# Moving the conditioning of layer B's gate from quarter 2 into quarter 1's output stage, in a two-layer fp32 decoder trunk

## The chip, the cores and the metric

The kernel runs on one core of one Trainium2 chip. The metric is the device time of one execution in microseconds (us), the median over several runs. The engines are named as the profile names them: PE is TensorE's matmul, PEld its weight load, DVE is VectorE, ACT is ScalarE, POOL is GpSimd, and SP is SyncE, whose queue issues every DMA of this kernel. TensorE's granted clock was 0.999 of full speed over the profiled execution, which is the 2.4 GHz level.

## The reference, cut to what matters

Layer A is a gated MLP with spatial mixing inside chunks of 128 tokens, layer B is dilated attention over a shared K/V. Both are conditioned by one vector `c`: a shift, a scale and a gate come from `silu(c) @ ada_w + ada_b`. This case is about layer B's gate, the last third of that product.

```
D_MODEL, SEQ, BATCH = 1024, 2048, 1

def ada_mod(c, w, b, n):
    h = jax.nn.silu(c) @ w + b
    return jnp.split(h[:, None, :], n, axis=-1)

def dilated_layer(x, c, kv_groups, ada_w, ada_b, norm_g, w_in, q_norm_g, w_out):
    shift, scale, gate = ada_mod(c, ada_w, ada_b, 3)
    h = rms_norm(x, norm_g) * (1 + scale) + shift
    ...
    y = o.reshape(bsz, s, B_WIDTH) * jax.nn.silu(z)
    return x + gate * (y @ w_out)
```

The gate of layer B is a row of 1024 numbers: a product of a vector of 1024 with a 1024 x 1024 block of `b_ada_w` (4.19 MB in fp32), plus a bias.

## The kernel before

The 2048 tokens are worked through in four quarters of 512 (`Q` = 0 to 3 in the code; "quarter 1" is `Q` = 0). Each quarter runs layer A and then the projections of layer B:

- the v blocks, with a gelu, then a spatial mix;
- the u and the z blocks (`dense_f`, 256 columns at a time);
- the output stage: `dense` over `a_w_out` in quarter 1, where each of two column halves `n` is made in two passes of 8 weight tiles (`kh`), so four passes in all. In later quarters it is a Strassen-like product, `dense_s`. Its result is gated, added to x, normalised and transposed;
- `proj_B`: the products for k and v (`kv_block` 2, 1, 0) and for q and z.

Dense work is in fp32r: each weight tile is loaded raw (`raw_o` and its like, 256 KB), ACT copies its high part into `w_o`, DVE subtracts that from the raw tile to get the low part (line 262), and PE runs three matmuls of 128x512 for each pair of tiles. There are 8 such split tiles (pool `wp`) and 6 raw ones (pool `rp`).

Beside the dense work run *fillers*: Python generators that emit side work in slices, in turn. `tick(part)` stands after each weight tile and adds `rate[0] * part` slices to a counter; `fill` pops the first generator of a list, advances it by one `yield` and puts it at the end. So the rate and the number of fillers set how fast each one is emitted. What is emitted is then ordered on each engine by a list scheduler at compile time: instructions keep a priority by the order in which they were emitted, a tile waits for a free buffer of its tag, and each engine, and SP's DMA queue, then runs its list strictly in order.

The fillers that matter here:

- `side_work` (quarter 1): layer A's gate, the shifts and scales, and `combine_weights` for layer B's input weights. It ends about where the output stage of quarter 1 begins.
- `combine_v` (quarter 1, from the output stage on): for 8 values of `k` it loads four 256 KB tiles of v's weights (line 378), combines them with four DVE subtractions (lines 382 to 385) and stores them to `wv` (line 256). Its tiles lie in the attention's buffers (`pr`, `pT`, `qt`, `qT`), which are idle until quarter 2. It takes 36 slices. `wv` is first read in quarter 2's v blocks.
- `attend_local` (from quarter 2 on): attention of groups 1 and 0 for the quarter before, and `combine_weights((4, 5), True)` for the output weights.
- `ada_gate(..., 1, "gb")`: layer B's gate. For each of two column halves `h`, `ada_acc` loads four tiles of 512 KB of `b_ada_w` (line 175) and accumulates eight 128x512 products on DVE (lines 177 and 179) into a tile of tag `ev` (pool `ep`, 6 buffers); six idle slices later PE sums over partitions (line 232, a 128x512 fp32 matmul with one stationary column), DVE adds the bias row (line 233) and SP stores the row to `gd`. One half is 10 slices, so the whole is 20. `gate_out`, in quarter 3, is the first to read it.

In quarter 2 the gate is woven into `attend_local`: `weave(main, side)` advances `side` once with each slice of `main`, and it has no slices of its own as long as `main` lasts. Its weight tiles take turns with the attention's `kv` tiles in pool `xp` (tag `xin`, 4 buffers).

Of the kernel before, what the change touches and what calls it, by code (L numbers as in the profile page):

```python
# [12 lines left out]
F32 = mybir.dt.float32  # L13
F32R = mybir.dt.float32r
AF = mybir.ActivationFunctionType
ALU = mybir.AluOpType
AX = mybir.AxisListType

P = 128
D = 1024  # L20
# [14 lines left out]
def trunk(ctx, tc, out, x, c, a_ada_w, a_ada_b, a_norm_g, a_w_in, a_sgu_g, a_w_spatial,  # L35
          a_b_spatial, a_w_out, kv_ada_w, kv_ada_b, kv_norm_g, w_kv, k_norm_g, b_ada_w,
          b_ada_b, b_norm_g, b_w_in, b_q_norm_g, b_w_out, dbg=None):
    nc = tc.nc
# [11 lines left out]
    xp = ctx.enter_context(tc.tile_pool(name="xp", bufs=4))  # L50
# [4 lines left out]
    ap_ = ctx.enter_context(tc.tile_pool(name="ap", bufs=2))  # L55
# [10 lines left out]
    wt = [[dp.tile([512, 512], F32, name=f"wt{b}_{i}") for i in range(4)] for b in range(4)]  # L66
# [8 lines left out]
    fillers = []  # L75
# [13 lines left out]
    rate = [0, 0]  # L89
# [7 lines left out]
    def drain():  # L97
        while fillers:
            fill(1)

    def evt(name, dt=F32):
        return ep.tile([P, 512], dt, tag="ev", name=name)

    def pst(name, tag="a"):
        return ps.tile([P, 512], F32, tag=tag, name=name)
# [26 lines left out]
    sc = cp.tile([P, KT], F32, name="sc")  # L132
# [33 lines left out]
                            channel_multiplier=-1)  # L166


    def ada_acc(res, w, c0, nm):

        acc = evt(f"acc_{nm}")
        for k in range(KT):
            if k % 2 == 0:
                wt = xp.tile([P, 2, 512], F32, tag="xin", name=f"aw_{nm}{k}")
                nc.sync.dma_start(wt, w[k * P:(k + 2) * P, c0:c0 + 512].rearrange("(k p) n -> p k n", p=P))
            if k == 0:
                nc.vector.tensor_scalar(acc, wt[:, 0, :], sc[:, 0:1], None, ALU.mult)
            else:
                nc.vector.scalar_tensor_tensor(acc, wt[:, k % 2, :], sc[:, k:k + 1], acc, ALU.mult, ALU.add)
            if k % 2:  # L180
                yield
        res.append(acc)
# [39 lines left out]
    def ada_gate(w, b, i, nm):  # L222
        for h in range(2):
            res = []
            cs = slice(h * 512, (h + 1) * 512)
            yield from ada_acc(res, w, 2 * D + h * 512, f"{nm}{h}")
            yield from [None] * (3 if i else 1)
            row = evt(f"gr_{nm}{h}")[0:1, :]
            nc.sync.dma_start(row, b[:, 2 * D + h * 512:2 * D + (h + 1) * 512])
            yield from [None] * 3  # L230
            pg = pst(f"pg_{nm}{h}")
            nc.tensor.matmul(pg[0:1, :], ones, res[0], start=True, stop=True)
            nc.vector.tensor_tensor(row, pg[0:1, :], row, ALU.add)
            nc.sync.dma_start(gd[i:i + 1, cs], row)
# [170 lines left out]
    def idle(n, gen):  # L405

        for _ in range(n):
            yield
        yield from gen

    def weave(main, side):

        for _ in main:
            next(side, None)
            yield
        for _ in side:
            yield
# [91 lines left out]
    def sum_tile(nm):  # L509
        return tp.tile([P, 516], F32, tag="st", name=f"st_{nm}")  # L510
# [492 lines left out]
    def layer_A(Q, hA, m, sqv, us=None, sums=None):  # L1003
# [69 lines left out]

        if Q == 0:
            fillers.append(combine_v())
            rate[0] = 1.6
        xts = []
        for t in range(TPQ):
            xt = xp.tile([P, D], F32, tag="xin", name=f"xr{Q}_{t}")
# [413 lines left out]
    def attend_local(Q, wrap=False):  # L1493

        bs = range(4 * Q, 4 * Q + 4)
        yield from attend([(1, b) for b in bs], wrap)
        v = stat[1][:, 4 * Q:4 * Q + 4, :]
        nc.sync.dma_start(std[1].rearrange("(n i r) c -> i n r c", n=4, r=4)[:, Q], v)
        yield
        nc.sync.dma_start(v, std[1].rearrange("(b i) c -> i b c", i=P)[:, 4 * Q:4 * Q + 4])  # L1500
        yield from attend([(0, b) for b in bs], wrap, 3)
# [205 lines left out]
    for Q in range(NQ):  # L1707
        if Q > 0:
            main = attend_local(Q - 1, True)
            if Q == 1:  # L1710
                fillers.append(weave(main, idle(12, ada_gate(b_ada_w[0], b_ada_b, 1, "gb"))))
                fillers.append(idle(8, combine_weights((4, 5), True)))
            else:
                fillers.append(weave(main, idle(16, gate_out())) if Q == 2 else main)
            rate[0] = 1.8 if Q == 1 else 0.6
        if Q == 0:
            with in_order(behind=True):
                hk, hb, keep, tail = layer_A(Q, hA, m, sqv, first)
        else:
            hk, hb, keep, tail = layer_A(Q, hA, m, sqv, sums=sums)  # L1720
        if Q > 0:
            drain()
        nxt = {}

        def ahead(Q=Q):
            if Q + 1 < NQ:
                fillers.append(make_hA(nxt, Q + 1, affa))
                rate[0] = 1.1
            else:
                nxt["fin"] = finish()  # L1730
            return nxt.get("fin")
        proj_B(Q, hk, hb, keep, tail, ahead)
        if Q + 1 < NQ:
            drain()
            hA, sums = nxt["hA"], nxt.get("ops")
            m, sqv = v_tiles(Q + 1)
# [23 lines left out]
```

## Time and profile before

| what | value |
|---|---|
| median of 3 runs | 2903.24 us (2902.45 to 2907.31) |
| the profiled execution | 2904.99 us |
| its span, first to last instruction | 2903.3 us |
| PE busy | 2875.6 us (99%) |
| PEld busy | 2419.2 us (83%) |
| DVE busy | 2219.1 us (76%) |
| ACT busy | 1667.6 us (57%) |
| DMA traffic | 693.82 MB, 239 GB/s over the span |

The profiled execution's own time is its span and 1.7 us around it. A busy PE need not be PE at its peak, since the ends of matmuls are modelled; so the count of matmuls in a stretch is read beside its busy time.

### The profile page before, as it was taken

Reading aid. Unit: us, or ns where it says so; the run is one execution under the profiler, and the core shown is the slowest. Engines: PE = TensorE matmul, PEld = TensorE weight load, DVE = VectorE, ACT = ScalarE, POOL = GpSimd, SP = SyncE. Lnnn points to the kernel's source line nnn. Section 1 sums busy time; section 2 is a strip of 40 time slices with the busy share of each in tenths; the row PEclk is TensorE's granted clock in tenths of the full one; section 3 lists DMA queues with packets and bytes.
Section 4 is the critical chain, followed back from the end, with each engine's and each line's share of the span. In section 5 each row is a group of like instructions: output and inputs, shape, how many; then the busy total and the mean of one; then the engine's idle time right before and its main releaser. Section 6 shows DMA issues by size and latency. Waiting matters only on the chain. (4 is left out here: it accounts for less than half of the span.)

```text
span 2903.3 us, 44921 instructions
## 1 busy us (share of the span) xinstructions
PE 2875.6 (99%) x14610; PEld 2419.2 (83%) x14610; DVE 2219.1 (76%) x4246; ACT 1667.6 (57%) x3400; POOL 258.2 (9%) x549
## 2 busy tenths in 40 slices
PE   8999999999999999999999999999999999999999
PEld 5888888888888888888888888888888888988887
DVE  6786677787758986887878876987678876888972
ACT  4423345668456765676555665676355667876540
POOL 1000001101011000000010000000010003311100
PEclk9999999999999999999999999999999999999999
DMA  7899788777998577776676676766554667889842
GB/s 258 298 311 297 265 287 292 241 250 249 311 334 284 171 259 225 239 247 201 212 262 198 192 253 212 243 225 197 172 174 155 223 219 238 269 265 340 260 144 87
DMA packets 390783, 693.82 MB, mean 239 GB/s; under 512 B 42027, under 2 KB 119821, under 8 KB 390549
## 3 DMA queue, kind: packets, MB, share of 16 engines
q1 hardware_dynamic: 390548, 690.97, 72.3%
q8 instruction: 115, 1.88, 0.3%
q14 instruction: 120, 0.98, 0.1%
HBM read 530.97 MB, written 159.85 MB: 238 GB/s over the span
## 5 line engine op out<-in xcount | busy, mean ns | idle before, releaser
L306 PE MATMUL pd_kv<-w_kv,hkh 128*128 128x512 f32 x768 | 238.5, 391 | 0.3 <-DMA w_kv<-wk 0.2
L355 PE MATMUL pd_u<-hAh,w_u 128*128 128x512 f32 x512 | 207.8, 406 | 0.0
L355 PE MATMUL pd_z<-hAh,w_z 128*128 128x512 f32 x512 | 205.8, 402 | 0.0
L1423 ACT ACTIVATE pr<-pr,stat,rt 128x256 f32<-128x256 f32 (+1 forms) x320 | 177.4, 556 | 45.3 <-DVE stat L1420 30.0
L357 PE MATMUL pd_u<-hAh,w_u 128*128 128x512 f32 x512 | 200.6, 392 | 1.7 <-DVE w_u L262 1.7
L357 PE MATMUL pd_z<-hAh,w_z 128*128 128x512 f32 x512 | 200.4, 392 | 0.0
L356 PE MATMUL pd_u<-hAl,w_u 128*128 128x512 f32 x512 | 200.0, 391 | 0.0
L356 PE MATMUL pd_z<-hAl,w_z 128*128 128x512 f32 x512 | 199.8, 390 | 0.0
L306 PEld LDWEIGHTS pd_kv<-w_kv,hkh 128*128 128x128 f32 x768 | 143.3, 188 | 30.1 <-ACT w_kv L260 0.6
L1484 PEld LDWEIGHTS po<-kv,pT 128*128 128x128 f32 x1200 | 147.6, 191 | 7.4 <-ACT pT L1321 1.2
L1484 PE MATMUL po<-kv,pT 128*128 128x128 f32 x1200 | 149.8, 275 | 1.0 <-ACT pT L1321 1.0
L306 PE MATMUL pd_kv<-w_kv,hkl 128*128 128x512 f32 x384 | 149.8, 390 | 0.0
L1351 POOL TENSOR_SCALAR rt<-qt 128x4 f32<-128x4 f32 x96 | 26.8, 279 | 1311.9 <-DMA qt<-qd 724.7
L1413 DVE SCALAR_TENSOR_TENSOR pr<-dist,rt,ps 128x256 f32<-128x256 f32 (+1 forms) x320 | 124.7, 431 | 22.4 <-PE ps L1409 10.4
L260 ACT ACTIVATE w_u<-raw_u 128x512 fp32r<-128x512 f32 x96 | 59.5, 628 | 142.4 <-PE pd_u L357 95.2
L260 ACT ACTIVATE w_o<-raw_o 128x512 fp32r<-128x512 f32 x104 | 64.2, 628 | 96.4 <-PE pd_o L306 37.8
L260 ACT ACTIVATE w_q<-raw_q 128x512 fp32r<-128x512 f32 x144 | 88.6, 628 | 49.9 <-PE pd_kv L306 9.9
L357 PEld LDWEIGHTS pd_u<-hAh,w_u 128*128 128x128 f32 x512 | 96.1, 188 | 23.9 <-DVE w_u L262 2.9
L357 PEld LDWEIGHTS pd_z<-hAh,w_z 128*128 128x128 f32 x512 | 96.1, 188 | 21.0
L355 PEld LDWEIGHTS pd_u<-hAh,w_u 128*128 128x128 f32 x512 | 96.5, 188 | 18.4 <-issue 1.7
L356 PEld LDWEIGHTS pd_z<-hAl,w_z 128*128 128x128 f32 x512 | 96.5, 188 | 17.6
L355 PEld LDWEIGHTS pd_z<-hAh,w_z 128*128 128x128 f32 x512 | 96.4, 188 | 17.4
(866 smaller groups left out, 7944.8 us busy)
## 6 DMA issues: line engine op xcount, KB each, us to landing
raw_q<-in_b_w_in_dram SPq DMA_DIRECT2D x144, 256.0 KB, 3.8
w_z<-wuz SPq DMA_DIRECT2D x64, 512.0 KB, 4.3
raw_o<-in_a_w_out_dram SPq DMA_DIRECT2D x104, 256.0 KB, 3.5
qt<-qd SPq DMA_DIRECT2D x96, 258.0 KB, 3.6
raw_v<-in_a_w_in_dram SPq DMA_DIRECT2D x96, 256.0 KB, 4.0
raw_u<-in_a_w_in_dram SPq DMA_DIRECT2D x96, 256.0 KB, 5.3
od<-ot SPq DMA_DIRECT2D x96, 256.0 KB, 2.5
raw_kv<-in_w_kv_dram SPq DMA_DIRECT2D x76, 256.0 KB, 4.7
```

Source lines behind the costliest of these rows:

```text
L260: nc.scalar.activation(hi, src, AF.Copy)
L306: last_mm[0] = nc.tensor.matmul(pt, a, u[:, w, :], start=f, stop=e, skip_group_check=more)
L355: nc.tensor.matmul(pts[i], wh, hh[:, k, :], start=k == 0, stop=False)
L356: nc.tensor.matmul(pts[i], wh, hl[:, k, :], start=False, stop=False)
L357: nc.tensor.matmul(pts[i], wl, hh[:, k, :], start=False, stop=k == KT - 1)
L1351: nc.gpsimd.tensor_scalar(rt[:, 12:16], u["qt"][:, 512:516], 1.0 / P, EPS, ALU.mult, ALU.add)
L1413: nc.vector.scalar_tensor_tensor(pr[:, i, :], dist3[:, d0:d0 + w], u["rt"][:, h:h + 1], psc[:, i, :], ALU.mult, ALU.add)
L1423: nc.scalar.activation(pr[:, i, :], pr[:, i, :], AF.Exp, bias=mneg[:, i:i + 1], scale=u["rt"][:, h:h + 1], accum_out=lsum[:, i:i + 1])
L1484: nc.tensor.matmul(po[:, h * P:(h + 1) * P], u["pT"][h // hp][:, h % hp, j, :], u["kv"][:, j, kh, 1, :], start=j == 0, stop=j == nk - 1)
```

## The change

Layer B's gate is no longer woven into quarter 2's attention. It becomes a filler of its own in quarter 1's output stage, behind four idle slices, beside `combine_v`, and the rate there rises from 1.6 to 3.8. Its weight tiles no longer come from `xin`: those of `k` = 0 and 4 go into the attention's `kT` tile (one buffer, 128x2x512, unused until quarter 2), those of `k` = 2 and 6 into two `st` tiles each (pool `tp`, 8 buffers), loaded by two DMAs of 256 KB in place of one of 512 KB.

```
-    def ada_acc(res, w, c0, nm):
+    def ada_acc(res, w, c0, nm, late_tile=False):
 
         acc = evt(f"acc_{nm}")
         for k in range(KT):
             if k % 2 == 0:
-                wt = xp.tile([P, 2, 512], F32, tag="xin", name=f"aw_{nm}{k}")
-                nc.sync.dma_start(wt, w[k * P:(k + 2) * P, c0:c0 + 512].rearrange("(k p) n -> p k n", p=P))
+                src = w[k * P:(k + 2) * P, c0:c0 + 512].rearrange("(k p) n -> p k n", p=P)
+                if late_tile and k % 4:
+                    ws = [sum_tile(f"aw_{nm}{k}{i}")[:, 0:512] for i in range(2)]
+                    for i in range(2):
+                        nc.sync.dma_start(ws[i], src[:, i, :])
+                else:
+                    wt = ap_.tile([P, 2, 512], F32, tag="kT", bufs=1, name=f"aw_{nm}{k}") if late_tile else \
+                        xp.tile([P, 2, 512], F32, tag="xin", name=f"aw_{nm}{k}")
+                    nc.sync.dma_start(wt, src)
+                    ws = [wt[:, i, :] for i in range(2)]
             if k == 0:
-                nc.vector.tensor_scalar(acc, wt[:, 0, :], sc[:, 0:1], None, ALU.mult)
+                nc.vector.tensor_scalar(acc, ws[0], sc[:, 0:1], None, ALU.mult)
             else:
-                nc.vector.scalar_tensor_tensor(acc, wt[:, k % 2, :], sc[:, k:k + 1], acc, ALU.mult, ALU.add)
+                nc.vector.scalar_tensor_tensor(acc, ws[k % 2], sc[:, k:k + 1], acc, ALU.mult, ALU.add)
             if k % 2:
                 yield
         res.append(acc)
@@ ada_gate
-            yield from ada_acc(res, w, 2 * D + h * 512, f"{nm}{h}")
+            yield from ada_acc(res, w, 2 * D + h * 512, f"{nm}{h}", i > 0)
@@ layer_A
         if Q == 0:
             fillers.append(combine_v())
-            rate[0] = 1.6
+            fillers.append(idle(4, ada_gate(b_ada_w[0], b_ada_b, 1, "gb")))
+            rate[0] = 3.8
@@ the loop over quarters
             if Q == 1:
-                fillers.append(weave(main, idle(12, ada_gate(b_ada_w[0], b_ada_b, 1, "gb"))))
+                fillers.append(main)
                 fillers.append(idle(8, combine_weights((4, 5), True)))
```

## Rows read from the trace of the kernel before

**Rows 1.** The page: busy time of each engine, and GB/s in 40 equal slices.
```profile
span 2903.3 us, 44921 instructions
PE 2875.6 (99%) x14610; PEld 2419.2 (83%) x14610; DVE 2219.1 (76%) x4246; ACT 1667.6 (57%) x3400; POOL 258.2 (9%) x549
...
GB/s 258 298 311 297 265 287 292 241 250 249 311 334 284 171 259 225 239 247 201 212 262 198 192 253 212 243 225 197 172 174 155 223 219 238 269 265 340 260 144 87
```

**Rows 2.** Busy time by stretch: two passes, output stage, kv_block 2, quarters 2 and 4.
```profile
core 0: us, PE busy (x) PEld busy (x) DVE busy (x) ACT busy (x) POOL busy (x), PEclk, DMA share, GB/s
320.20:342.00 21.80, 21.80 (x98) 18.06 (x97) 16.75 (x27) 7.84 (x14) 0.00 (x0) 1.00 0.93 303
342.00:363.80 21.80, 21.80 (x98) 18.06 (x97) 8.15 (x13) 6.17 (x12) 0.00 (x0) 1.00 0.37 119
320.20:407.20 87.00, 87.00 (x393) 72.04 (x392) 50.84 (x82) 26.36 (x51) 2.40 (x4) 1.00 0.72 244
407.20:440.00 32.80, 32.25 (x150) 26.26 (x149) 31.81 (x57) 25.07 (x52) 2.94 (x4) 1.00 0.92 311
620.00:820.00 200.00, 197.30 (x1004) 163.82 (x1003) 151.35 (x271) 131.12 (x266) 14.84 (x26) 1.00 0.85 288
1860.00:2060.00 200.00, 200.00 (x1041) 170.21 (x1040) 160.41 (x309) 135.66 (x261) 17.03 (x34) 1.00 0.63 205
```

**Rows 3.** Waits of PE, 300 to 620 us and 620 to 820 us: total, times, longest.
```profile
PE pt_b L656 <- DVE xr L1106: 0.5, 1, 0.5
...
PE pd_u L357 <- DVE w_u L262: 1.7, 2, 1.0
PE pd_v10a L306 <- DVE w_v L262: 1.0, 2, 0.8
```

**Rows 4.** Instructions of lines 175, 177, 179, 232: ns min/median/max, first and last start.
```profile
L175 SPq DMA_DIRECT2D aw_gb<-in_b_ada_w_dram x8: 379/404/462, 647.3 to 774.1; - x8
DMA to landing us min/median/max: 3.8/5.6/9.9
L177 DVE TENSOR_SCALAR acc_gb<-aw_gb,sc x2: 478/478/478, 699.1 to 766.6; 128x512 f32<-128x512 f32 x2
L179 DVE SCALAR_TENSOR_TENSOR acc_gb<-aw_gb,sc,acc_gb x14: 731/740/752, 702.1 to 781.4; 128x512 f32<-128x512 f32 x14
L232 PE MATMUL pg_gb<-acc_gb,ones x4: 590/591/592, 764.1 to 810.6; 128*1 128x512 f32 x4
```

**Rows 5.** Timeline of quarter 2, 715 to 727 us: start, duration, idle before and releaser.
```profile
721.21 0.75 DVE L179 SCALAR_TENSOR_TENSOR acc_gb<-aw_gb,sc,acc_gb 128x512 f32<-128x512 f32 x1 [3.63 <-DMA aw_gb<-in_b_ada_w_dram]
...
725.67 0.69 DVE L262 TENSOR_TENSOR w_u<-raw_u,w_u 128x512 fp32r<-128x512 f32 x1
...
726.42 0.50 PE L357 MATMUL pd_u<-hAh,w_u 128*128 128x512 f32 x1 [1.00 <-DVE w_u L262]
```

**Rows 6.** Timeline of quarter 1's output stage, PE and DVE: start, duration, idle before.
```profile
320.19 0.61 PE L306 MATMUL pd_o<-w_o,yh 128*128 128x512 f32 x2
...
341.95 0.61 PE L306 MATMUL pd_o<-w_o,yh 128*128 128x512 f32 x2
342.81 0.69 DVE L262 TENSOR_TENSOR w_o<-raw_o,w_o 128x512 fp32r<-128x512 f32 x1 [0.62 <-ACT w_o L260]
...
366.27 0.68 DVE L262 TENSOR_TENSOR w_o<-raw_o,w_o 128x512 fp32r<-128x512 f32 x1
...
377.80 0.69 DVE L382 TENSOR_TENSOR co<-co,co 128x512 f32<-128x512 f32 x1 [7.56 <-DMA co<-in_a_w_in_dram]
378.41 0.68 DVE L262 TENSOR_TENSOR w_o<-raw_o,w_o 128x512 fp32r<-128x512 f32 x1
```

**Rows 7.** Waits of SP's DMA queue, 300 to 500 us, the first.
```profile
SPq L267 <- DVE w_o L262: 32.3, 18, 11.8
```

**Rows 8.** Instructions on combine_v's tiles of odd k: ns min/median/max, first and last start.
```profile
L378 SPq DMA_DIRECT2D co<-in_a_w_in_dram x16: 327/565/1212, 322.9 to 462.4; - x16
L382 DVE TENSOR_TENSOR co<-co,co x4: 681/688/692, 331.0 to 466.7; 128x512 f32<-128x512 f32 x4
```

## The prediction, made before the change was run

> **What bounds the kernel now.** I read the page first: PE is busy for 2875.6 of 2903.3 us, DVE for 2219.1 [rows 1]. A busy PE may still be a slow one, so I went to the busy times by stretch. The reader should see there that PE's pace does not depend on the side work: the first pass of quarter 1's output stage holds 98 matmul records in 21.8 us while DVE is busy for 16.75 us and the DMA engines for 0.93 of the time, and the second holds the same 98, with the same 18.06 us of weight loads, while DVE is busy for 8.15 us and DMA for 0.37 [rows 2]. The clock is 1.00 throughout, the 2.4 GHz level. So PE is the bound, and a change beside it can give back only what PE loses to waits, or add to it.
>
> Hence the list of PE's waits, for the stretch that gains work and the one that loses it. From 300 to 620 us it names one, of 0.5 us; in the output stage itself, 320.2 to 407.2 us, PE is busy for all 87.00 us [rows 2, 3]. From 620 to 820 us, where the gate lies now, it names 2.7 us in four waits, all on DVE's low parts of weights (line 262), and PE is idle there for 200 - 197.30 = 2.7 us too [rows 2, 3]. That is the whole prize in quarter 2. The bound I use for a change that can be measured here is 0.2%, 5.8 us.
>
> **What is removed.** The gate's work in quarter 2 is 8 loads of 512 KB (0.40 us of SP's queue each, landing after 5.6 us, 9.9 at most), 2 x 0.48 + 14 x 0.74 = 11.3 us of DVE, and two PE products, each of two records of 0.59 us [rows 4]. DVE is busy for 151.35 of 200 us there [rows 2], so its time lies in gaps; what can reach PE is a wait. The timeline shows one: DVE stood 3.63 us for a gate tile until 721.21 us, the split behind it came at 725.67, and PE waited for a split from 725.4 to 726.42 us, 1.00 us [rows 5]. The other 1.7 us have no such stop in front of them in these rows: 1.0 is in v's blocks, 0.7 is the second wait of u's [rows 3]. So I take -1.0 us, with 0 and -2.7 as ends: 0 if another late tile takes the gate's place in front of the split, -2.7 if a lighter queue cures all four. That `kv` tiles find `xin` free sooner I cost at nothing: no wait of PE there names the attention. Its slices of emission stay as they are, since `weave` gave the gate none of its own.
>
> **What is added in quarter 1.** The two PE products move with the rest and cost the same: 0. The loads become 4 of 512 KB and 8 of 256 KB, so four more issues at about 0.4 us of SP's queue, 1.6 us; the bias rows and their stores move unchanged. DVE gets the gate's 11.3 us. The slices: the stage has 64 ticks of 0.25, so 64 x 0.25 x 3.8 = 60.8 in place of 25.6. The gate needs 4 + 20 and one to end, and `side_work` has some 5 left: a third each of the first 15 slices, then half each, so the gate ends after 15 + 40 = 55 slices, inside the stage. `combine_v` gets 5 + 20 + 5, about 30, in place of 25.6 - 5, about 20: 10 more, or 2.5 values of `k`: 2.5 x 4 x 0.69 = 6.9 us of DVE [rows 8] and 2.5 x 2.1 = 5.2 MB, drawn forward out of the projections.
>
> DVE in the stage: 50.84 + 11.3 + 6.9 = 69 of 87 us [rows 2]. It fits. DMA: 87 us at 244 GB/s is 21.2 MB; with 4.2 and 5.2 it is 30.6 MB, or 352 GB/s, above the fastest fortieth of the span, 340 [rows 1, 2]. So the stage fills the DMA engines, and some 1 MB spills past its end, 3 us. What hides this is the lead of the weights. The passes begin at 320.19 and 341.95 us, 21.76 apart, and each works through its 8 tiles in the first 10.9 us, 1.36 us a tile. The last split of the second pass's tiles is ready at 343.5 us and wanted at 341.95 + 7 x 1.36 = 351.5: a lead of 8.0 us. The third pass begins at 363.7, its last split is ready at 366.95 and wanted at 373.2: 6.3 us [rows 6]. And a wait of the new kind has been there without harm: DVE stood 7.56 us for a tile of `combine_v`, the split behind it came at 378.41, was ready at 379.1, and was wanted at 385.5 [rows 6]. I take 0 for the stage, between 0 (all waits stay inside the lead, as that one did) and +9.8 us (worked out under the second rival).
>
> Behind the stage, in `kv_block` 2, DVE is busy for 31.81 of 32.8 us and PE idle for 0.55 [rows 2]. `combine_v` leaves it in part, so I take -0.5 us; the ends are -0.55 and, if half of the gate (5.7 us of DVE) were late enough to land there instead, 5.7 - 0.99 = +4.7 us.
>
> **The sum.** -1.0 + 0 + 0 - 0.5 = -1.5 us on the profiled execution's 2904.99, so 2903.5. The median of the runs is 1.75 us under that execution; as a median I predict 2903.24 - 1.5 = 2901.7 us.
>
> **Rivals.** *The first: Quarter 2 gains more than its named waits.* The share of weight loads is 163.82 of 200 us there and 170.21 in quarter 4's same blocks [rows 2]. If all of the difference were lost pace, 6.4 us at 0.851 per us is 7.5 us, and the median 2903.24 - 7.5 - 0.5 = 2895.2. Against it: quarter 4 has a different attention, so another mix of matmuls, and the two passes above kept their 18.06 us at very different loads. The Trainium skill ("Trainium Kernel Development and Optimization", Performance Expectations) says that matmul busy time misleads and that the busy share of weight loads is the measure; by that rule the 83% would leave room, and the time would be this rival's. The equal counts of the two passes speak against reading it so here.
>
> *The second, and the other side: a late gate tile holds the splits.* The place is DVE's list in the output stage. SP's queue stands up to 11.8 us at a time until a raw buffer is free, 32.3 us in 18 waits [rows 7]. A gate load queued behind such a wait, and landing after 9.9 in place of 5.6 us [rows 4], comes 11.8 + 4.3 = 16.1 us late; DVE stands for it, the splits stand behind it, and PE loses what is beyond the lead: 16.1 - 6.3 = 9.8 us. It decides from a wait of 6.3 us on. The single `kT` buffer makes it likelier: `k` = 4 can't be loaded until `k` = 1 has been used, and SP stands for that with the raw loads behind it. The median would be 2901.7 + 9.8 = 2911.5. For it: the 7.56 us wait, already over the smallest lead; in quarter 2 the same tiles made a stop of 3.63 us. Against it: that wait cost nothing, and the second pass has 13.65 us of free DVE. The Trainium skill ("TensorE: Matmul & The Clock Gate", the section on the 16 sub-arrays) gives VectorE a strictly ordered queue of 8. The split that came 0.6 us after the held subtraction agrees; by that rule the change moves a stop, it doesn't dissolve it.
>
> *The third: the move is less than it says.* The list scheduler may place the gate's second half in `kv_block` 2, where DVE has 0.99 us free: -1.0 + 4.7 = +3.7, so 2906.9. It is inside 0.2%. Any new order of the lists elsewhere (PE's whole idle time is 2903.3 - 2875.6 = 27.7 us over the span [rows 1]) I count into the spread.
>
> **How the numbers follow.** Forecast 0.72; larger gain 0.08; late tile 0.12; half move 0.08. The range: the forecast's own ends are -2.7 - 0.55, so 2900.0, and with the 0.8 us between the two lower runs 2899.2; above, 2906.9 is the third rival. For the cases beyond I open it to 2898 and 2909, which takes in a small version of each. Faster by over 0.2% is the first rival, 0.08; slower is the second, 0.12; the forecast and the third rival are within, 0.80.
>
> **What would show it.** Right: no `acc_gb` after some 405 us, PE's 1.00 us wait at 726 us gone, PE busy for all of the output stage with 393 records in 87 us, DVE near 69 us there, DMA share over 0.9. Wrong: waits of PE on `w_o` in the output stage, behind a stop of DVE over 6.3 us on an `aw_gb` tile; or `acc_gb` beside `kv_block` 2 and PE waiting for `hkl` or `w_kv`; or quarter 2's weight loads rising toward 170 us in 200.

## The result, and the profile after

The change made the kernel slower: a median of 2924.66 us (2921.49 to 2929.91, 6 runs) against 2906.72 us for the kernel before in the same comparison (2902.45 to 2907.31, 6 runs, the three of the table of before among them). The ratio is 1.0068, with a 95% interval of 1.0055 to 1.0081. The prediction was 2901.7 us, with a range from 2898 to 2909. In the new file the lines up to 1073 stand 8 lower and the later ones 9 lower: the low part of a weight is line 270, the matmul of `dense` is line 314, `combine_v`'s four subtractions are lines 390 to 393.

The head of the page answers to [rows 1]:

```profile
span 2921.6 us, 44949 instructions
PE 2883.1 (99%) x14610; PEld 2422.2 (83%) x14610; DVE 2221.7 (76%) x4246; ACT 1670.4 (57%) x3400; POOL 263.2 (9%) x549
```

The span grew by 18.3 us. PE's idle time went from 27.7 to 2921.6 - 2883.1 = 38.5 us, so 10.8 of them are waits. The other 7.5 us are PE being busy for longer over the same 14610 instructions. The busy times by stretch say where (columns as in [rows 2]):

```profile
320.00:340.00 20.00, 14.90 (x57) 11.80 (x57) 15.20 (x26) 4.67 (x9) 0.00 (x0) 0.86 0.95 316
340.00:360.00 20.00, 20.00 (x87) 16.47 (x86) 9.59 (x15) 5.06 (x8) 0.00 (x0) 0.97 0.84 272
...
400.00:420.00 20.00, 16.45 (x72) 13.41 (x71) 10.96 (x19) 4.27 (x9) 2.56 (x4) 0.91 0.93 342
620.00:820.00 200.00, 200.00 (x1018) 169.14 (x1017) 151.37 (x268) 139.60 (x278) 13.91 (x26) 1.00 0.86 287
```

Two things are new in quarter 1's output stage: PE is idle, and the granted clock is below 1.00. Over 20 us that is a mean; in two shorter stretches the granted clock was 0.50, the level of 1.2 GHz:

```profile
334.50:341.30 6.80, 5.80 (x14) 4.55 (x15) 5.92 (x10) 1.63 (x3) 0.00 (x0) 0.50 0.85 260
416.50:419.90 3.40, 3.40 (x13) 2.81 (x12) 1.70 (x3) 0.63 (x1) 0.00 (x0) 0.50 0.61 211
```

At 1.00 the stage's rate is 90 records in 20 us (98 in 21.8 us, [rows 2]). The first two rows hold 57 + 87 = 144 in place of 180, which is 36 x 0.222 = 8.0 us. PE's waits from 300 to 470 us answer to the one of 0.5 us in [rows 3]:

```profile
PE pd_o L314 <- DVE w_o L270: 5.1, 1, 5.1
PE pt_b L664 <- DVE xr L1115: 3.5, 1, 3.5
```

So of the 8.0 us 5.1 are the wait and 2.9 the slower clock, which is half of the 5.80 busy us at 0.50. The second wait is 3.5 us, and half of 3.40 busy us at 0.50 is 1.7 us more. Quarter 2, in the last row of the stretches, has lost its idle time: 200.00 us busy in place of 197.30.

What stood ahead of the first wait is in the timeline of DVE, with PE's matmul that ended it:

```profile
324.04 0.69 DVE L390 TENSOR_TENSOR co<-co,co 128x512 f32<-128x512 f32 x1 [1.06 <-DMA co<-in_a_w_in_dram]
324.64 1.28 DVE L270 TENSOR_TENSOR w_o<-raw_o,w_o 128x512 fp32r<-128x512 f32 x2
329.33 0.69 DVE L391 TENSOR_TENSOR co<-co,co 128x512 f32<-128x512 f32 x1 [3.40 <-DMA co<-in_a_w_in_dram]
329.94 3.70 DVE L1078 TENSOR_TENSOR yl<-mt,yh 128x512 fp32r<-128x512 f32 x6
333.55 1.28 DVE L1071 TENSOR_TENSOR mt<-mt,z 128x512 f32<-128x512 f32 x2
334.76 0.68 DVE L270 TENSOR_TENSOR w_o<-raw_o,w_o 128x512 fp32r<-128x512 f32 x1
...
335.50 0.79 PE L314 MATMUL pd_o<-w_o,yh 128*128 128x512 f32 x1 [5.10 <-DVE w_o L270]
```

The reader is to see which tile DVE stood for: `co`, a tile of `combine_v`, and not one of the gate's. Behind it stood 5 us of other work (lines 1078 and 1071), which stands ahead of that split in the kernel before too, and behind that the last split of the first pass. The second wait has the same kind of cause; these are DVE's rows ahead of the scaled rows `xr` that PE transposes:

```profile
403.64 0.69 DVE L390 TENSOR_TENSOR co6pr<-co6pr,co6pr 128x512 f32<-128x512 f32 x1 [4.59 <-DMA co6pr<-in_a_w_in_dram]
...
413.18 0.69 DVE L390 TENSOR_TENSOR co<-co,co 128x512 f32<-128x512 f32 x1 [3.06 <-DMA co<-in_a_w_in_dram]
...
415.14 0.75 DVE L1115 TENSOR_SCALAR xr<-xr,r_b 128x1024 f32<-128x1024 f32 x1
```

The gate itself ran as predicted. Its instructions by line answer to [rows 4], and its last product on DVE begins at 389.2 us, before the forecast's 405:

```profile
L187 DVE SCALAR_TENSOR_TENSOR acc_gb<-st_aw_gb,sc,acc_gb x8: 744/750/752, 339.1 to 389.2; 128x512 f32<-128x512 f32 x8
L187 DVE SCALAR_TENSOR_TENSOR acc_gb<-aw_gb,sc,acc_gb x6: 744/750/754, 337.6 to 387.6; 128x512 f32<-128x512 f32 x6
L240 PE MATMUL pg_gb<-acc_gb,ones x4: 590/590/591, 384.5 to 423.2; 128*1 128x512 f32 x4
```

**Four stretches, all kernels.** One profiled execution varies, so the table splits each by the first matmul of a tile: "stage" from the first of `pd_o` to the first of `pd_kv`, "behind" from there to the first of `pd_q00a`, "quarter 2" from `pd_v10a` to `pd_o1a`, "later" from `pd_o1a` to `pf`, in us. The ratio is that of the timed runs, against runs of the kernel before in the same comparison. Names are those of the experiments below.

| kernel | stage | behind | quarter 2 | later | ratio (95%) |
|---|---|---|---|---|---|
| before | 88.9 | 144.3 | 318.7 | 1674.1 | |
| after | 104.7 | 143.5 | 312.2 | 1682.3 | 1.0068 (1.0055 to 1.0081) |
| gate alone, rate 1.6 | 92.5 | 147.6 | 312.1 | 1672.8 | 1.0002 (0.9991 to 1.0013) |
| rate 3.8 alone | 99.2 | 144.2 | 316.7 | 1681.7 | 1.0060 (1.0042 to 1.0078) |
| no gate | 90.8 | 144.4 | 312.1 | 1672.8 | 0.9981 (0.9972 to 0.9990) |
| combine_v 6 slices later | 94.3 | 145.4 | 313.0 | 1679.5 | 1.0028 (1.0018 to 1.0038) |
| remainder alone | 89.3 | 145.5 | 315.8 | 1677.5 | 1.0042 (1.0025 to 1.0058) |
| remainder set back | 106.3 | 143.4 | 313.1 | 1672.2 | 1.0046 (1.0029 to 1.0063) |
| first pass at 1.6 | 101.1 | 144.8 | 312.4 | 1673.8 | 1.0041 (1.0026 to 1.0056) |
| late combine_v and gate | 94.0 | 144.8 | 312.1 | 1670.5 | 1.0007 (0.9998 to 1.0017) |
| after, combine_v on POOL | 100.6 | 143.6 | 312.2 | 1678.0 | 1.0050 (1.0035 to 1.0066) |
| the same, remainder set back | 101.1 | 145.4 | 312.1 | 1673.3 | 1.0032 (1.0020 to 1.0043) |
| before, combine_v on POOL | 89.0 | 147.6 | 315.8 | 1673.7 | 1.0019 (1.0009 to 1.0029) |
| gate alone, combine_v on POOL | 90.6 | 152.3 | 312.1 | 1671.4 | 1.0009 (0.9999 to 1.0018) |
| no k = 1 subtractions | 104.8 | 143.5 | 312.2 | 1681.3 | 1.0071 (1.0056 to 1.0086) |
| gate twice per slice | 91.4 | 143.4 | 314.0 | 1675.3 | 1.0000 (0.9991 to 1.0010) |
| old pace of combine_v | 97.0 | 144.7 | 311.9 | 1670.6 | 1.0021 (1.0011 to 1.0030) |

The stage has the same order of instructions on DVE and SP in "before", "no gate" and "remainder alone": 88.9, 90.8 and 89.3 us, so it is read to about 2 us. Nor is the profiled run always near the median of its kernel: with the remainder alone it took 2911.10 us (median 2918.38), with the old pace of `combine_v` 2903.39 (2908.74), with the gate twice per slice 2907.81 (2903.65). After against before: +15.8 in the stage, -0.8 behind it, -6.5 in quarter 2, +8.2 later. With what lies between, it makes the 18.3 us of the span.

### The profile page after: what moved, and what is told of

The parts are those of the page before. It is cut to its first block, busy times and chain, and to the rows that moved or that the text cites. A ratio compares the mean times of both kernels' runs of the same rounds, so it can differ in the third digit from the quotient of the medians.

```text
span 2921.6 us, 44949 instructions
## 1 busy us (share of the span) xinstructions
PE 2883.1 (99%) x14610; PEld 2422.2 (83%) x14610; DVE 2221.7 (76%) x4246; ACT 1670.4 (57%) x3400; POOL 263.2 (9%) x549
## 4 chain that ended last, share of the span: by engine, by line
PE 78%; DMA 9%; DVE 6%; ACT 3%; issue 2%; SPq 1%; POOL 0%; DVEq 0%; ACTq 0%; POOLq 0%
PE pd_kv L314 9%; PE po L1493 4%; PE pd_u L363 4%; PE pd_u L365 4%; PE pd_u L364 4%; PE pd_z L363 3%; PE pd_z L365 3%; PE pd_z L364 3%; PE pd_v L314 2%; PE pm L1038 2%; PE pf L1689 2%; PE pf L1688 2%; PE pf L1687 2%; PE pd_o3a L314 1%; PE pd_o2b L314 1%
## 5 line engine op out<-in xcount | busy, mean ns | idle before, releaser
L365 PEld LDWEIGHTS pd_u<-hAh,w_u 128*128 128x128 f32 x512 | 96.1, 188 | 20.8
L364 PEld LDWEIGHTS pd_u<-hAl,w_u 128*128 128x128 f32 x512 | 96.5, 189 | 17.1
```

The lines of the kernel that those rows point to most:

```text
L364: nc.tensor.matmul(pts[i], wh, hl[:, k, :], start=False, stop=False)
L365: nc.tensor.matmul(pts[i], wl, hh[:, k, :], start=False, stop=k == KT - 1)
```

## The experiments

**1. The two halves of the change by themselves.** The first kernel has the gate in the new place at the old rate, the second the new rate with the gate left in quarter 2.

```
+            fillers.append(weave(combine_v(), idle(4, ada_gate(b_ada_w[0], b_ada_b, 1, "gb"))))
             rate[0] = 1.6
```
```
             fillers.append(combine_v())
-            rate[0] = 1.6
+            fillers.append(idle(24, iter(())))
+            rate[0] = 3.8
```

> The gate moves into the output stage and the attention's buffers as in the change, but the rate stays at 1.6 and the gate is woven into the combining of v's weights, so that this keeps the slices it had before. Theory A (the higher rate pulls the combining's subtractions ahead of weight splits; the gate itself is harmless): no wait of PE on a weight split near 330 us and none on the normalised rows near 415, quarter 1 ends within 2 us of before, quarter 2 gains some 5 us, and the time is between 2898 and 2906, ratio 0.997 to 1.001. Theory B (the gate's own tiles and traffic hold the splits): waits of PE of 3 us or more in the output stage with gate instructions in front of the split, and 8 us or more over before.

> The gate stays in quarter 2 as before; in the output stage the rate is 3.8 and an empty filler of 24 slices takes the turns that the gate would have had, so that the combining of v's weights runs at the changed kernel's pace without the gate. Theory A: the same wait of some 5 us near 330 us behind a subtraction that waits for its load, quarter 1 some 8 to 15 us longer than before, and since quarter 2's gain is missing, 10 to 20 us over before (ratio 1.003 to 1.007). Theory B: quarter 1 within 2 us of before, the time within 0.2% of before.

Measured: 2906.21 us (ratio 1.0002) for the gate, 2923.99 us (1.0060) for the rate. The rate alone is about as slow as the changed kernel, without a gate in the stage. Its DVE and its PE show the same kind of stop:

```profile
333.58 0.69 DVE L383 TENSOR_TENSOR co<-co,co 128x512 f32<-128x512 f32 x1 [4.70 <-DMA co<-in_a_w_in_dram]
...
339.00 0.68 DVE L262 TENSOR_TENSOR w_o<-raw_o,w_o 128x512 fp32r<-128x512 f32 x1
...
339.74 0.80 PE L306 MATMUL pd_o<-w_o,yh 128*128 128x512 f32 x1 [6.73 <-DVE w_o L262]
```

In the stage the rate costs 99.2 - 88.9 = 10.3 us and the gate 92.5 - 88.9 = 3.6; both together cost 15.8, which is 1.9 us more and within the 2 us to which the stage is read. With the gate alone quarter 2 is 6.6 us shorter too; the kernel comes out level because its stage is 3.6 us longer and the stretch behind it 3.3 (147.6 in place of 144.3). The reason for the rate's cost is in the order in which the compiled program lists DVE's work; the trace of each kernel has DVE's instructions in that order. These are the kernel before (first) and after (second), from the fifth split of the first pass to its last; the numbers are places in the list:

```
358 L262 TENSOR_TENSOR w_o_0_4_2850<-raw_o_0_4_2851,w_o_0_4_2850 128x512
359 L262 TENSOR_TENSOR w_o_0_5_2855<-raw_o_0_5_2856,w_o_0_5_2855 128x512
360 L262 TENSOR_TENSOR w_o_0_6_2860<-raw_o_0_6_2861,w_o_0_6_2860 128x512
361 L1070 TENSOR_TENSOR yl_2418<-mt_1_1121,yh_2417 128x512 x6
362 L1063 TENSOR_TENSOR mt_1_1121<-mt_1_1121,z_14_2805 128x512
363 L1063 TENSOR_TENSOR mt_1_1121<-mt_1_1121,z_15_2810 128x512
364 L262 TENSOR_TENSOR w_o_0_7_2865<-raw_o_0_7_2866,w_o_0_7_2865 128x512
```
```
358 L270 TENSOR_TENSOR w_o_0_4_2850<-raw_o_0_4_2851,w_o_0_4_2850 128x512
359 L390 TENSOR_TENSOR co_2990<-co_2991,co_2990 128x512
360 L270 TENSOR_TENSOR w_o_0_5_2855<-raw_o_0_5_2856,w_o_0_5_2855 128x512
361 L270 TENSOR_TENSOR w_o_0_6_2860<-raw_o_0_6_2861,w_o_0_6_2860 128x512
362 L391 TENSOR_TENSOR co_2991<-co_2992,co_2991 128x512
363 L1078 TENSOR_TENSOR yl_2418<-mt_1_1121,yh_2417 128x512 x6
364 L1071 TENSOR_TENSOR mt_1_1121<-mt_1_1121,z_14_2805 128x512
365 L1071 TENSOR_TENSOR mt_1_1121<-mt_1_1121,z_15_2810 128x512
366 L270 TENSOR_TENSOR w_o_0_7_2865<-raw_o_0_7_2866,w_o_0_7_2865 128x512
```

The higher rate emits `combine_v`'s `k` = 1 earlier, and two of its subtractions come to stand ahead of `w_o_0_7`. Before, all four stood behind it.

**2. No gate at all, and combine_v held back.** The first kernel shows what is to be had at most; it leaves the gate of layer B out. The second is the changed kernel with six idle slices ahead of `combine_v`.

```
-            fillers.append(idle(4, ada_gate(b_ada_w[0], b_ada_b, 1, "gb")))
-            rate[0] = 3.8
+            rate[0] = 1.6
```
```
-            fillers.append(combine_v())
+            fillers.append(idle(6, combine_v()))
```

> Layer B's gate is not computed at all (the gated output weights take layer A's gate row in its place); everything else, rate included, is as before. This prices what leaving quarter 2 can give at most, under both theories: between -7 and 0 us against before, with PE's losses between 620 and 820 us down from some 5 us to 1. If it is slower than before, or if later quarters lose several us, then the order of later instruction lists moves the time by itself, whatever is taken out.

> The change with one addition: the combining of v's weights starts six slices later, so that none of its subtractions stands ahead of the first pass's last weight split. Theory A: the wait of 5.1 us near 330 us is gone and the clock stays at 1.00 there, 8 us less than the changed kernel in that pass; the second stop, near 412 us, may stay, since the combining still runs at the high rate. So 2908 to 2918. Theory B: the gate's own instructions stand where they stood, so both stops stay, 2920 or more.

Measured: 2900.25 us (0.9981) without a gate, and 2913.53 us (1.0028) with `combine_v` later. So all of the gate's work is worth 0.19%, some 5.5 us, and that is the most that any place for it could give. The gate's products take 2.4 us of PE in any place, so if PE stays the bound, some 3 us are left to be won, 0.1%. Holding `combine_v` back took 104.7 - 94.3 = 10.4 us out of the stage and PE's wait on `w_o` away altogether; the wait for `xr` kept 2.7 us; it is the only wait of PE from 300 to 460 us. The later quarters stayed at 1679.5 us.

```profile
PE pt_b L664 <- DVE xr L1115: 2.7, 2, 2.5
```

**3. The remainder of the slice counter.** The later quarters lose some 8 us although nothing in their code was changed. `tick` adds `rate[0] * part` to `rate[1]` and keeps the fraction. The stage's 64 ticks of 0.25 add 25.6 at rate 1.6 and 60.8 at 3.8; the fraction left over is 0.2 larger, is never set back, and from there on some slices are emitted one tick sooner. One kernel is before with 0.2 added, the other after with 0.2 taken off.

```
         rate[0] = 1.7
+        if Q == 0:
+            rate[1] += 0.2        # the other kernel: rate[1] += -0.2
         prs, hooks = tail
```

> The kernel before, with one number changed: at the start of proj_B of quarter 1 the counter of slices gets 0.2 added. 64 ticks of 0.25 at rate 3.8 leave a remainder 0.2 larger than at rate 1.6, and the counter is never set back, so every later quarter emits some of its slices one tick earlier. Theory C: this remainder is the cause of what quarters 2 to 4 lost in the changed kernel. Then quarter 1 and its output stage stay as they were (first matmul of pd_q00a within 1 us), three losses of some 3 us each appear behind it (from pd_o1a to pd_q10a, from pd_v20a to pd_o2a, from pd_v30a to pd_o3a), and the time is some 9 us above the kernel before. Rival D: the later losses come from what quarter 1's stage left behind (order of buffers, stores of wv); then this kernel stays within 0.1% of before.

> The changed kernel, with 0.2 taken off the counter at the start of proj_B of quarter 1, so that the later quarters emit at the ticks of the kernel before. Theory C: the stops of the output stage stay (pd_q00a +15 us), quarter 2 gives its 6.6 back, and nothing is lost from there on: some 8 to 9 us above before, about 2914. Rival D: the time of the changed kernel, 2924.

Measured: 2918.38 us (1.0042) and 2917.95 us (1.0046). Adding 0.2 to one number made the kernel before slower by 0.42%, with its stage as it was. Taking it off brought the changed kernel from 1.0068 to 1.0046. Over all profiles "later" parts cleanly: 1677.5 to 1682.3 us in the six kernels with the shifted remainder (mean 1680.1), 1670.5 to 1675.3 in the eleven others (mean 1672.8). So it costs 7.3 us in the profiles; the timed ratios, 0.42% and 0.22%, put it at 12 and 6 us. The profile of the remainder alone is that of its fastest run, 7 us below its median. With the remainder alone PE waits at the start of quarter 4's v blocks, 1850 to 2250 us, where the kernel before names no wait:

```profile
PE pd_v30a L306 <- ACT m L811: 2.5, 1, 2.5
PE pd_v30a L306 <- DVE w_v30t L262: 0.4, 1, 0.4
PE pd_v30a L306 <- ACT st_v30u L587: 0.3, 1, 0.3
PE pd_v31a L306 <- DVE w_v31t L262: 0.2, 1, 0.2
```

Of the three losses of 3 us that were expected, that profile shows 4.5 us in quarter 4 (`pd_v30a` to `pd_o3a`), 1.0 in quarter 2 and none in quarter 3, so the size per quarter is not settled. In the changed kernel the same three stretches are 3.1, 3.4 and 3.2 us longer than before.

**4. Is it only the first pass?** The changed kernel with the first pass at 1.6 and the others at 3.8, and a version meant to be better, with `combine_v` held for 10 slices and a middle rate. In both the rates are chosen so that the remainder is that of before.

```
+            rate[0] = paces[kh] if paces else rate[0]      # in dense, per pass
-            dense(yT, a_w_out, n * 512, f"o{Q}{n}", ev)
+            dense(yT, a_w_out, n * 512, f"o{Q}{n}", ev, paces=(1.6, 3.8, 3.8, 3.95)[2 * n:2 * n + 2])
```
```
+            fillers.append(weave(idle(10, combine_v()), idle(2, ada_gate(b_ada_w[0], b_ada_b, 1, "gb"))))
+            dense(yT, a_w_out, n * 512, f"o{Q}{n}", ev, paces=(1.6, 3.225, 3.225, 1.6)[2 * n:2 * n + 2])
```

> The changed kernel with the old rate of 1.6 in the first pass alone, 3.8 in the second and third and 3.95 in the fourth (the remainder is that of the kernel before, so nothing is lost in the later quarters if theory C holds). Theory A: the stop of 5.1 us at 335 us is gone with the slower clock behind it; the stop of 3.5 us at 415 us, where a tile of combine_v stands ahead of the scaled rows, stays or moves. So pd_q00a at +4 to +8 us, and with quarter 2's 6.6 given back 2903 to 2908. Theory B: the gate's tiles are now all in the passes at the high rate and hold the splits there: PE waits on w_o in the second or third pass, 2912 or more.

> A version meant to be better than both: the gate woven into combine_v, combine_v held for 10 slices, the gate for 2, and the rate 1.6 in the first and last pass and 3.225 in the two between (the sum of slices leaves the remainder of the kernel before). Theory A (a stop of DVE costs only where the lead of the splits is short, in the first pass, and where combine_v is pulled forward): no wait of PE on w_o over 1 us, the gate's last acc_gb before 408 us, pd_q00a at +3 us or less, the 6.6 us of quarter 2 given back, so 2899 to 2903. Theory B (the gate's own tiles hold the splits): waits of PE on w_o in the second and third pass, and 2908 or more.

Measured: 2917.13 us (1.0041) and 2907.55 us (1.0007). Both are misses, the first by 9 us and the second by 4.6. The stop at 335 us is gone, but PE waits 1.9 us for a split at 376 us and 4.7 us for `xr`; ahead of them DVE had stood 7.38 and 4.55 us for `combine_v` tiles. The first of the two has a share of the gate in it: between the 7.38 us and that split DVE ran seven of the gate's products and stood 1.36 us for a gate tile. The kernel with the remainder set back and 3.8 throughout took 1.0046, so slowing the first pass alone is worth nothing that can be seen in the time (the stages are 101.1 and 106.3 us). The second has the stage at 94.0 us and ends level with before.

**5. The subtraction's place, or the traffic?** First `combine_v`'s subtractions went to POOL, so that DVE never stands for its tiles: in the changed kernel, in the one with the remainder set back, in before, and in the gate alone.

```
-            nc.vector.tensor_tensor(t1, t3, t1, ALU.subtract)        # and the other three
+            nc.gpsimd.tensor_tensor(t1, t3, t1, ALU.subtract)
```

> The changed kernel with combine_v's four subtractions issued on POOL in place of DVE; its loads, its pace and the gate are as in the changed kernel. Theory A1: it is the place of a late combine_v tile in DVE's list that costs, since the splits stand behind it. Then the 5.1 us wait of PE on w_o goes (under 1.5 us), though the tiles land as late and the DMA share is as high. The wait for the scaled rows may stay, since their factor r_b is made on POOL, behind the same subtractions. First matmul of pd_q00a at +4 to +9 us in place of +15.3, time 2912 to 2918. Theory A2: it is the traffic itself, the raw weights landing late; then PE waits as long as in the changed kernel and the time stays at 2922 or more.

> The kernel of the run with the remainder set back (counter less 0.2 at proj_B of quarter 1), and combine_v's subtractions on POOL. By theories A1 and C together both of its losses are gone but for the wait for the scaled rows: 2904 to 2910. By A2 it stays at 2917 or more.

> The kernel before with combine_v's subtractions on POOL alone, the control for the two runs above. In before no wait of PE stands behind combine_v but for 0.5 us, so by A1 nothing is gained: within 0.1% of before. If POOL's work slows DVE, or POOL holds r_b behind a late tile, it is slower by some 3 us.

> The gate woven into combine_v at the old rate 1.6 (so neither slices nor remainder change), and combine_v's subtractions on POOL. This is the version from which the most is to be hoped: quarter 2's 6.6 us stay given back, of which 2.4 are the gate's own products that quarter 1 now pays, and DVE has 22 us less to do beside the gate. By A1 2898 to 2903, below before by up to 0.2%; if the remaining waits of the gate in kv_block 2 were not DVE's load, as in the run with the gate alone, 2906.

Measured: 2918.67 us (1.0050), 2913.13 us (1.0032), 2909.36 us (1.0019) and 2907.49 us (1.0009). Each is above what theory A1 gave. The wait on `w_o` fell from 5.1 to 1.0 us in the first, but was 6.0 us in the second, whose order on DVE is the same there. So this did not settle it: the edit does more than free DVE, as DVE's rows of the first kernel show (the second of these lines is POOL's):

```profile
317.83 6.89 DVE L270 TENSOR_TENSOR w_o<-raw_o,w_o 128x512 fp32r<-128x512 f32 x4
...
320.85 1.62 POOL L392 TENSOR_TENSOR co0pT<-co0pT,co0pr 128x512 f32<-128x512 f32 x1
```

Four splits took 6.89 us, 1.72 us each, in place of some 0.65 us (two in 1.28 us, above), as long as POOL worked beside them. The Trainium skill ("SBUF — State Buffer", Who interferes with whom) says that a DVE instruction with two SBUF inputs contends with a GpSimd instruction that reads SBUF; these rows agree. The control was slower than before by 0.19%; its stage is as long as before (89.0 us), and the stretch behind it, where `combine_v` goes on, is 3.3 us longer (147.6 us). The gate alone with POOL has 152.3 us there.

The cleaner cut leaves the four subtractions of `k` = 1 out and keeps every load: SP's list through the stage is that of the changed kernel.

```
-            if k < KT:
+            if k < KT and k != 1:
                 combine(k)
```

> The changed kernel without the four subtractions of combine_v's k = 1 (that part of v's weights is stored uncombined, so part of the computation is left out). Every load and store stays: SP's list is that of the changed kernel through the output stage; in DVE's list the four subtractions, two of which stood ahead of the last split of the first pass, are gone. Theory A1 (the place in the list): the 5.1 us wait of PE on w_o and the lower clock behind it are gone, the 3.5 us stop at 415 us stays; pd_q00a +6 to +10 in place of +15.3, time 2913 to 2919. Theory A2 (the traffic): the wait stays at 4 us or more and the time at 2921 or more.

Measured: 2923.35 us (1.0071). The wait went as theory A1 said, the time as theory A2 did: the stop and the clock fall that came with it are gone from the first two passes, and the loss is not. Its stretches, PE's waits from 300 to 470 us, and DVE's row ahead of the longest one:

```profile
320.00:340.00 20.00, 19.30 (x86) 15.64 (x85) 12.85 (x21) 8.56 (x15) 0.00 (x0) 1.00 0.98 341
340.00:360.00 20.00, 19.41 (x86) 15.76 (x85) 12.39 (x19) 1.90 (x3) 0.00 (x0) 1.00 0.89 296
360.00:380.00 20.00, 16.68 (x67) 13.32 (x66) 12.13 (x21) 7.40 (x16) 0.00 (x0) 0.91 0.85 298
```
```profile
PE pt_b L664 <- DVE xr L1115: 4.7, 1, 4.7
PE pd_o L314 <- DVE w_o L270: 4.6, 3, 3.3
```
```profile
368.00 0.69 DVE L390 TENSOR_TENSOR co<-co,co 128x512 f32<-128x512 f32 x1 [5.47 <-DMA co<-in_a_w_in_dram]
```

For the first stop the place in the list is shown: with the same loads and without those subtractions PE waits 0.7 us there in place of 5.1. But the stage takes 104.8 us, against 104.7 in the changed kernel. PE came earlier to the next late tile of `combine_v` and waited 3.3 us there, the clock fell to 0.91 behind it, and the wait for `xr` grew from 3.5 to 4.7. Taking one stop away moved the loss; with the slow first pass the stops moved too, and 12.2 of the stage's 15.8 us stayed.

**6. The rate, or what it pulls forward?** The last two kernels keep `combine_v` at its old pace: one with the rate of 3.8, the other with the old rate and the gate at two steps per slice, begun five slices late.

```
+            fillers.append(slower(combine_v()))      # two steps in three slices; remainder set back
             fillers.append(idle(4, ada_gate(b_ada_w[0], b_ada_b, 1, "gb")))
             rate[0] = 3.8
```
```
+            fillers.append(weave(combine_v(), idle(5, twice(ada_gate(b_ada_w[0], b_ada_b, 1, "gb")))))
             rate[0] = 1.6
```

> The changed kernel at rate 3.8 with combine_v slowed to two steps in three slices, which gives it the pace of the kernel before, and with the remainder set back. The gate runs at its fast pace. Theory A: it was combine_v pulled forward; both stops go, and the time is that of the gate alone at the old rate, 2902 to 2908. Theory B, or that the fast rate harms by the gate's own pace: PE waits on w_o in the first or second pass for 3 us or more, and 2912 or more.

> A version meant to beat both: old rate 1.6, the gate woven into combine_v, five slices late and then two steps per slice, so that combine_v, the remainder and the first pass stay as in the kernel before, and the gate's loads fall at 335 to 345 us, where the DMA share of before is 0.31. Theory A: no wait of PE over 1 us in the output stage; quarter 1 pays the gate's four products, 2.4 us, and quarter 2 gives back 6.6; so about 4 us below before, 2899 to 2903. If the gate's tiles hold the splits (theory B), 2907 or more.

Measured: 2908.74 us (1.0021) and 2903.65 us (1.0000). At the same rate and with the same gate, the old pace of `combine_v` took the stage from 106.3 to 97.0 us, and the median from 2917.95 to 2908.74 us. What is left is a wait of 2.4 us for `xr`, behind a `combine_v` tile for which DVE stood 6.20 us, and one of 1.3 us for a split, behind a stop of 2.63 us for a gate tile and one of 2.58 us for a tile of `combine_v`:

```profile
PE pt_b L671 <- DVE xr L1122: 2.4, 1, 2.4
PE pd_o L314 <- DVE w_o L270: 1.3, 1, 1.3
```

The second kernel has no wait of PE at all from 300 to 470 us, while DMA moved 293 GB/s in the first 80 us of the stage, where before it moved 235 (the DMA share of before from 335 to 345 us is 0.77, and not the 0.31 of the expectation, which is that from 340 to 360):

```profile
320.00:400.00 80.00, 80.00 (x351) 65.30 (x350) 55.19 (x87) 23.15 (x42) 0.00 (x0) 1.00 0.86 293
```

So the gate can lie in the stage without a stop. A gain does not show even so: the ratio's interval is 0.1% to either side, and the 3 us to be won are no more than that.

## Why the prediction was wrong

**The step that failed is the output stage, "I take 0 for the stage, between 0 ... and +9.8 us".** It measured +15.8 us, of which the gate's four products are 4 x 0.59 = 2.4; they moved from quarter 2, as the prediction had it. So the term of 0 was 13.4 us: two waits of 5.1 and 3.5 us, and 2.9 and 1.7 us lost to the granted clock of 0.50, 13.2 by these rows. Three things went wrong in that step.

- *The lead.* It was taken from the second and third pass, 8.0 and 6.3 us. The first pass was not worked out. By the same rule its last split was wanted at 320.19 + 7 x 1.36 = 329.7 us, and in the kernel before it begins here:

```profile
327.86 0.69 DVE L262 TENSOR_TENSOR w_o<-raw_o,w_o 128x512 fp32r<-128x512 f32 x1
```

  It was ready at 328.5, so the lead was 1.2 us, and it is no more than that: in the kernel without a gate, where DVE has the same order, PE waits 1.5 us for this split:

```profile
333.32 0.50 PE L314 MATMUL pd_o<-w_o,yh 128*128 128x512 f32 x1 [1.48 <-DVE w_o L270]
```

  In the changed kernel two waits, 1.06 and 3.40 us, and two subtractions of 0.69 us stand ahead of it: 5.8 us, of which 4.6 are over the lead, and PE waited 5.1. The 7.56 us wait that "cost nothing" lay behind the third pass's last split (366.27 us) and ahead of the fourth's first, which was still ready 6.4 us before it was wanted: it came where some 14 us were to spare, and says nothing of the last split of a pass.
- *What the rate pulls forward.* The prediction counted it rightly: 10 slices more for `combine_v`, 2.5 values of `k`. From 300 to 422 us the changed kernel begins all 8 values on DVE and ends 7; before it begins 6 and ends 5. But it was priced as 6.9 us of DVE time and 5.2 MB, and both fit. What cost is the place: a pulled subtraction stands in front of weights, on an engine that runs its list strictly in order, and DVE stands there until its tile has landed.
- *The clock.* No term held it. In the kernel before PE's longest wait from 300 to 470 us is 0.5 us [rows 3]; here each of the two stops came with a stretch at 0.50: 4.6 us in all.

**The second rival had the right mechanism and the wrong tile.** It gave a late *gate* tile in front of the splits 0.12 and 9.8 us. The tiles ahead of the changed kernel's two waits are `combine_v`'s. The gate alone costs the stage 3.6 us, with 1.4 us as its longest wait on `w_o` (1.5 us without any gate), and 91.4 - 88.9 = 2.5 in the kernel with two steps per slice, of which 2.4 are its products. Gate tiles have a part in two small waits only: the 1.9 us with the slow first pass and the 1.3 us with the old pace of `combine_v`. The Trainium skill ("TensorE: Matmul & The Clock Gate", the section on the 16 sub-arrays), as the prediction has it, says that VectorE's queue is strictly ordered. The rows agree: in the changed kernel and with the rate alone the last split of the first pass stood behind a held subtraction. That the change would move a stop, as the prediction inferred, fell short: it made stops that the stage did not have.

**Quarter 2 was about right.** Four profiles with the gate there take 318.7, 316.7, 315.8 and 315.8 us, the thirteen without it 311.9 to 314.0 (mean 312.4). The mean difference is 4.3 us, less 2.4 of moved products 1.9: inside the forecast's 0 to 2.7, above its 1.0. On the two profiles compared first it is 6.5 - 2.4 = 4.1 us, since before had the longest of the four. The 2.7 us of named waits are all gone. The first rival, 7.5 us by the share of weight loads, falls: that share rose from 163.82 to 169.14 of 200 us, near quarter 4's 170.21, but quarter 2 gained 1.9 us on the mean, not 7.5, once the moved products are taken off.

**The term behind the stage** was -0.5: from the first matmul of `pd_kv` to that of `pd_q00a` it is 143.5 us in place of 144.3, so -0.8. The third rival, half of the gate in `kv_block` 2, did not happen in the changed kernel. It did in the gate alone at rate 1.6, where the second half's products on DVE run up to 428.5 us and this stretch is 3.3 us longer than before; the rival's price for it was 4.7.

**One term was missing.** "Any new order of the lists elsewhere" was left to the spread. It was 7.3 us, more than quarter 2's whole gain, and came from a fraction of 0.2 in a counter. That fraction could have been seen before the run, since 60.8 and 25.6 stand in the prediction side by side; its price could not.

The sum of the measured terms, -1.9 + 13.4 - 0.8 + 7.3 = 18.0 us, is the 17.9 us between the medians. That it comes so near is luck: the stage alone is read to 2 us.

What stays open is why one tick makes the later quarters slower (only that it does was shown), and why some tile of `combine_v` is late in each pass at rate 3.8. For the first stop the rows narrow it. The first line is SP's, from the changed kernel; the others are the loads with the same `k` in the kernel before, of which two have a landing on record:

```profile
323.06 0.90 SPq L386 DMA_DIRECT2D co<-in_a_w_in_dram  x2
```
```profile
L378 SPq DMA_DIRECT2D co<-in_a_w_in_dram x4: 476/590/707, 322.9 to 325.8; - x4
DMA to landing us min/median/max: 6.6/6.7/6.8
```

The tile that DVE stood for until 329.33 us was issued at 323.06 or later, so it landed at most 6.3 us after its issue, no later than before. It was issued earlier than before, where the last of these loads went out at 325.8 us, but DVE came to it earlier still: at 325.9 us in place of 331.7. So a slower landing is not the cause there, and heavy traffic alone makes no stop: the kernel with 293 GB/s has none. What the traffic does to the later tiles was not tested; no run here changed the traffic and kept the lists.

## What to carry to other kernels

When the pace of side work goes up, work out the lead of the weights in each pass, the first above all, and ask which of the side work's instructions will come to stand ahead of them on an engine that runs in order; free time of that engine says nothing about this. A wait taken away at one late tile can be paid at the next, so test the change that delays or thins the late tiles and not the one that removes a stop. And when a rate or a counter is changed, look for what it carries over into code that was not touched, or set it back.

## What the runs showed of the hardware that was not expected

- PE stood from 330.4 to 335.5 us in a full stretch, and the granted clock was 0.50 from 334.5 to 341.3 us; it stood 3.5 us until 416.0 us, and the clock was 0.50 from 416.5 to 419.9. The clock's price was about half of the stop's. The length of the wait does not tell by itself whether the clock falls: after 2.38 us for `xr` (old pace of `combine_v`) it was 0.50 from 408.5 to 411.9 us, after 2.49 us for `xr` (`combine_v` 6 slices later) it stayed at 1.00. The first of these rows is from the former, the second from the latter:

```profile
408.50:411.90 3.40, 3.40 (x12) 2.71 (x11) 1.76 (x4) 0.63 (x1) 0.00 (x0) 0.50 0.91 310
405.00:415.00 10.00, 7.51 (x38) 5.31 (x38) 9.40 (x18) 5.68 (x12) 2.35 (x4) 1.00 0.94 341
```

- Subtractions on POOL slowed DVE's beside them from some 0.65 to 1.72 us each, and took POOL 1.62 us in place of DVE's 0.69. With the side work on POOL the kernel before was slower by 0.19%.
